# Late stores and the modulation's weight loads issued from GpSimd's queue instead of SP's, in a kernel of two transformer-like blocks

## The chip, the cores and the metric

The kernel runs on one core of a Trainium2 chip. The metric is the device time of the core in microseconds, from launch to end, the median of several runs; lower is better. TensorE multiplies matrices, VectorE (DVE) and ScalarE (ACT) work on whole tiles of 128 partitions, GpSimd (POOL) does the same more slowly, and SyncE (SP) does nothing but issue DMA transfers. An engine works through its own instructions in order; an instruction waits until the semaphores of those that it depends on are set. Every engine can issue transfers, and a transfer's issue instruction stands in the queue of the engine that issues it, so that it waits there for its data and holds up what is behind it.

## The reference

Two blocks in float32 over x [1024 tokens, 1024 features]. The first: a norm, one wide projection, a bidirectional gated delta rule with 4 heads beside windowed attention with sinks, both gated, and an output projection added to x. The second has a modulation: from a condition c, six vectors of 1024 (shift, scale and gate for the attention, and the same for the feed-forward).

```python
x = x + mix @ w_out                                   # first block's end
mod = silu(c) @ w_ada + b_ada                         # w_ada [1024, 6144]
sh1, sc1, g1, sh2, sc2, g2 = split(mod, 6)
h = rms_norm(x, norm1_g) * (1 + sc1) + sh1
gq, gk, gv, gr, glr, aq, ak, av = split(h @ w_in)
y_gla = gated_linear_attention(gq, gk, gv, gr, glr)
y_att = dilated_attention(rms_norm(aq), rms_norm(ak), av)   # 8 heads, 3 dilations
x = x + g1 * (concat(y_gla, y_att) @ w_out_2)
h = rms_norm(x, norm2_g) * (1 + sc2) + sh2
u = causal_conv(h @ w_up)                             # 2 x 2816 wide
x = x + g2 * ((silu(u_gate) * u_val) @ w_down)
```

## The kernel before

Activations lie transposed, features on partitions, as 128x512 tiles (two halves of the 1024 tokens). Every float32 product is made of three passes: each operand is split into a high part (ACT) and a low part (DVE), and TensorE adds high x high, high x low and low x high (mm3, L217 to L221). So each weight tile goes through a load, an ACT split and a DVE split (load_piece, L204 to L211: the load at L208 into one of two "wr" tiles, the splits at L209 and L210 into one of eight "wh" and "wl" tiles).

The stages, by the profile's times: first projections to 360 us; delta rule and windowed attention to 620; output projection 1 (out_proj, L322 to L393) to 727; second projections to 1105; dilated attention as filler from about 880 and the gated linear attention to 1285; output projection 2 to 1378; the up projection in 22 steps to 1800; the down projection to the end.

Transfers are issued in three queues, named at L117: `dma` is SP's, `store` is ACT's, `pdma` is POOL's. Before the change POOL's queue issues only the 28 stores of the delta rule's preparation (L678, L687, L714) between 258 and 321 us; nearly all others are SP's. The order in which each engine issues its instructions is not that of the program's text: a scheduler of the language lays it out ahead, with a timeline of its own, so that a transfer which moves to another queue can change the order elsewhere too. Transfers of one queue also rotate over completion semaphores, eight for the hardware queues and eight others for POOL's.

The places that the change touches:

- `ada` (L395 to L414) makes the modulation. Each of 12 steps j sums eight products of a 128x512 weight tile with a per-partition scalar: the first tile is loaded into the accumulator aac (L401) and scaled by ACT (L405), the other seven tiles wa are loaded (L401) and added by DVE (L403); then four small matmuls sum over partitions (pada, L412), and L414 puts the result into mods. Steps 0 to 3 run as filler in output projection 1; steps 4 to 11 are interleaved with the start of the second projections, two loads per step, with four 256 KB tiles for accumulator and weights together.
- L863 stores the delta rule's output yt (two buffers) to DRAM, 16 times 128 KB.
- `evac1` (L1080) adds output projection 1 to x and stores x1, 16 times 256 KB (L1082). The norm behind it (fin1, L1086 to L1093) scales x in place (L1088) and makes the second projections' inputs ho.
- L1260 stores a quarter of a head of the dilated attention, yd with one buffer, 32 times 64 KB; L1277 reads them back for output projection 2.
- `evac2` (L1620) and L1622 do for output projection 2 what evac1 does, with the modulation's gate: 16 stores of x2.
- `gated` (L1706) stores the activation of each of the 22 steps of the up projection, 512 KB each (L1721).

The up weights come in at L1576 (wu), are split at L1579 and L1580; the b tiles (b30l, b60l and so on) are sums of activations for the up projection's products, their low parts made at L1736. L1308 squares a tile of q or k on POOL for its norm, L1157 works on rotated q. L361 loads weights of the output projections (rawo, rawp).

Of the kernel before, what the change touches and what calls it, by code (L numbers as in the profile page):

```python
# [22 lines left out]
P = 128  # L23
# [89 lines left out]
def tile_two_blocks(ctx: ExitStack, tc: tile.TileContext, t, out, dbg=None, stop=None):  # L113
# [3 lines left out]
    dma, store, pdma = nc.sync.dma_start, nc.scalar.dma_start, nc.gpsimd.dma_start  # L117
# [18 lines left out]
    def after(*names):  # L136

        c = ExitStack()
        for n in names:
            c.enter_context(tc.issue_after(marks[n].ins))  # L140
        return c
# [253 lines left out]
    def ada(page, pbank, js):  # L395

        for j in js:
            aac = page("aac", f"aac{j}")
            for k in range(NK):
                wa = page("wa", f"wa{j}_{k}") if k else aac  # L400
                dma(wa, t["w_ada_2"][j, k])  # L401
                if k:
                    V.scalar_tensor_tensor(aac, wa, silc[:, k : k + 1], aac, ALU.mult, ALU.add)  # L403
                else:
                    A.activation(aac, aac, AF.Copy, scale=silc[:, 0:1])  # L405
                yield
            for _ in range(ADA_D):
                yield
            with after("mm3"):
                ps = pbank(f"pada{j}", [P, 4])  # L410
                for i in range(4):
                    T.matmul(ps[:, i : i + 1], aac[:, i * P : (i + 1) * P], ones, start=True, stop=True)  # L412
            md = mods[:, j // 2, 4 * (j % 2) : 4 * (j % 2) + 4]
            V.tensor_tensor(md, ps, md, ALU.add)  # L414
# [3 lines left out]
    ydram = scratch("ydram", [512, S])  # L418
# [4 lines left out]
    x1dram, x2dram = scratch("x1dram", [D, S]), scratch("x2dram", [D, S])  # L423
    mix = [[None, None] for _ in range(NK)]

    with ExitStack() as c1:
# [28 lines left out]
        with ExitStack() as ca:  # L455
# [4 lines left out]
            def page(tag, name, shape=None, dt=F32):  # L460
                return ga.tile(shape or [P, H], dt, name=name, tag=tag, bufs=BUFS_A[tag])
# [327 lines left out]
        with ExitStack() as cb_:  # L789
# [47 lines left out]
            def swa_values(b, g, sts, zt):  # L837
                kb0, kb1 = max(b - 1, 0), min(b + 2, NB)
                nm_ = f"{b}{g}"
                pts = []  # L840
                for i, kb in enumerate(range(kb0, kb1)):
                    pt = pb("pt", f"pT{nm_}{kb}", G4)
                    for h in range(4):
                        T.transpose(pt[:, h, :], sts[h][:, i * P : (i + 1) * P], ident)
                    pT = page("pTs", f"pTs{nm_}{kb}")
                    if PTS[kb % len(PTS)]:
                        A.activation(pT, pt, AF.Copy)
                    else:
                        V.tensor_copy(pT, pt)  # L849
                    pts.append(pT)  # L850
                    yield
                po = pb("po", f"po{nm_}", [P, 4, 64])
                for h in range(4):
                    for i, kb in enumerate(range(kb0, kb1)):
                        T.matmul(po[:, h, :], pts[i][:, h, :], sv[:, kb, g * 64 : (g + 1) * 64], start=i == 0, stop=kb == kb1 - 1)  # L855
                V.tensor_tensor(zt, zt, po, ALU.mult)
                yield
                pt = pb("pt", f"yp{nm_}", [P, 2, P])
                for i in range(2):
                    T.transpose(pt[:, i, :], zt[:, 2 * i : 2 * i + 2, :].rearrange("p a b -> p (a b)"), ident)  # L860
                yt = pg.tile([P, 2, P], F32, name=f"yt{nm_}", tag="wa", bufs=2)
                A.activation(yt, pt, AF.Copy)
                dma(ydram[g * 256 : (g + 1) * 256, b * P : (b + 1) * P].rearrange("(i p) s -> p i s", p=P), yt)  # L863
                yield

            def swa():
# [211 lines left out]
    with ExitStack() as co:  # L1078

        def evac1(xr, ps, m, cols):  # L1080
            V.tensor_tensor(xr, ps, xr, ALU.add)
            dma(x1dram[m * P : (m + 1) * P, cols], xr)  # L1082

        hs = [[None, None] for _ in range(NK)]

        def fin1(h, xs, rows, gsc, xp):  # L1086
            for k in range(NK):
                A.activation(xs[k], xs[k], AF.Copy, scale=gsc[:, k : k + 1])  # L1088
                V.tensor_tensor(xs[k], xs[k], rows, ALU.mult)
                hi, lo = hpage(f"ho{h}{k}h"), hpage(f"ho{h}{k}l")  # L1090
                A.activation(hi, xs[k], AF.Identity, bias=mods[:, 0, k : k + 1])
                V.scalar_tensor_tensor(lo, xs[k], mods[:, 0, k : k + 1], hi.bitcast(F32), ALU.add, ALU.subtract)
                hs[k][h] = (hi, lo)  # L1093

        order = (4, 5, 6, 7, 0, 1, 2, 3)
        ppo = pool(co, "ppo", space=PSUM)

        def modulation(xp):

            tiles = lambda tag, nm: xp.tile([P, H], F32, name=nm, tag=tag, bufs=dict(aac=2, wa=6)[tag])  # L1100
            return ada(tiles, lambda nm, shape: ppo.tile(shape, F32, name=nm, tag="nm", bufs=2), range(4))

        out_proj(co, ppo, t["w_out"], mix, t["xT"], evac1, "norm1_g_2", 0, "o", order, fin1, lambda: swa_mix(1), filler=modulation)
        free("O1")
        dump("x1", x1dram)
# [5 lines left out]
    yadram = scratch("yadram", [512, S])  # L1111
    mixg = [[None, None] for _ in range(4)]
    mixa = [[None, None] for _ in range(4)]
    with ExitStack() as c2:
# [75 lines left out]
        def attend(h, ready):  # L1190

            qs, kT, tb, vv, _ = ready
            for j in LASTJ if h == 7 else range(NB // 2):
# [58 lines left out]
                yd = rd = page("yd", f"ayd{h}{j}", [64, 2 * P])  # L1252
# [3 lines left out]
                else:  # L1256
                    A.activation(rd, po[64:128, : 2 * P], AF.Copy)
                    V.tensor_tensor(yd, po[0:64, : 2 * P], rd, ALU.add)
                    V.tensor_tensor(yd, yd, po[0:64, 2 * P :], ALU.mult)
                dma(yadram[h * 64 : (h + 1) * 64, j * 2 * P : (j + 1) * 2 * P], yd)  # L1260

        def heads(h0, h1):
            ready = {h0: prep(h0)}
# [19 lines left out]
        with ExitStack() as ca:  # L1283
# [120 lines left out]
            for nm in JOBS.split():  # L1404
                g = int(nm[-1])
# [159 lines left out]
    adram2 = scratch("adram2", [DFF, S])  # L1565
    with ExitStack() as cf:
# [52 lines left out]

        def evac2(xr, ps, m, cols):  # L1620
            V.scalar_tensor_tensor(xr, ps, mods[:, 2, m : m + 1], xr, ALU.mult, ALU.add)
            dma(x2dram[m * P : (m + 1) * P, cols], xr)  # L1622

        with after("exp", "red"):
            for j in range(2):
# [83 lines left out]
        def gated(j):  # L1709

            us = []
            c1, c2 = quarters.pop(j)
            for m, cc, tg in ((NFF + j, c2, "u"), (j, c1, "act")):
                u = page4(tg, f"u{m}", [P, S])
                A.activation(u, cc, AF.Identity, bias=fcb[:, m : m + 1], scale=fcw[:, m, 2:3])  # L1715
                for sft in (1, 2):
                    V.scalar_tensor_tensor(u[:, sft:], cc[:, : S - sft], fcw[:, m, 2 - sft : 3 - sft], u[:, sft:], ALU.mult, ALU.add)  # L1717
                us.append(u)
            A.activation(us[1], us[1], AF.Silu)
            V.tensor_tensor(us[1], us[1], us[0], ALU.mult)  # L1720
            dma(adram2[j * P : (j + 1) * P, :], us[1])  # L1721

        fcw = load(fw, "fcw", [P, 2 * NFF, 3], t["conv_w_2"])
        fcb = load(fw, "fcb", [P, 2 * NFF], t["conv_b_2"])
# [49 lines left out]
        for j in range(2):  # L1774
            gated(j)
# [55 lines left out]
        w1, w2, b = {}, {}, {}  # L1831
# [9 lines left out]
        for q in PROD_D:  # L1841
# [38 lines left out]
            for m in range(4):  # L1880
                p = ps[m]
# [3 lines left out]
                else:  # L1885
# [5 lines left out]
                    g, h = {2: (0, 0), 4: (1, 0), 5: (1, 1), 3: (0, 1)}[q]  # L1891
                    xr, dst = final(g, m, h, c, f"{q}{m}")
# [94 lines left out]
```

## Time and profile before

| | us |
|---|---|
| median of 3 runs | 2028.75 |
| lowest, highest | 2025.3, 2029.26 |
| the profiled execution | 2027.4 |
| its span, first to last instruction | 2025.6 |
| TensorE busy | 1938.5 |
| DVE busy | 1457.2 |
| ACT busy | 952.8 |
| POOL busy | 334.0 |
| mean granted clock | 0.978 |

TensorE's busy time is that of matmuls, which are pipelined. An issue instruction of a transfer is not counted as busy, so that a full queue of SP doesn't show in these numbers; it shows in the waits of SP's queue and in its timeline. Each wait is listed with what ended it.

### The profile page before, as it was taken

Reading aid. Unit: us, or ns where it says so; the run is one execution under the profiler, and the core shown is the slowest. Engines: PE = TensorE matmul, PEld = TensorE weight load, DVE = VectorE, ACT = ScalarE, POOL = GpSimd, SP = SyncE. Lnnn points to the kernel's source line nnn. Section 1 sums busy time; section 2 is a strip of 40 time slices with the busy share of each in tenths; the row PEclk is TensorE's granted clock in tenths of the full one; section 3 lists DMA queues with packets and bytes.
Section 4 is the critical chain, followed back from the end, with each engine's and each line's share of the span. In section 5 each row is a group of like instructions: output and inputs, shape, how many; then the busy total and the mean of one; then the engine's idle time right before and its main releaser. Section 6 shows DMA issues by size and latency. Waiting matters only on the chain.

```text
span 2025.6 us, 31441 instructions
## 1 busy us (share of the span) xinstructions
PE 1938.5 (96%) x11430; PEld 1683.3 (83%) x11430; DVE 1457.2 (72%) x3031; ACT 952.8 (47%) x1982; POOL 334.0 (16%) x389
## 2 busy tenths in 40 slices
PE   7999999899989998899999899999999999999999
PEld 6988889889977788798999787786888888888887
DVE  6797885587886478544354978449977777776987
ACT  6546563243353152125644566436554544554443
POOL 0000021563351123021022742110000000000000
PEclk9999999999999989899999999999999999999999
DMA  5232343325428327633222222611222222268332
GB/s 176 71 105 69 89 148 118 78 59 184 134 89 312 120 92 241 205 118 92 74 73 82 59 71 81 227 63 59 84 73 94 83 73 94 73 208 281 99 99 84
DMA packets 175996, 234.74 MB, mean 116 GB/s; under 512 B 57024, under 2 KB 93152, under 8 KB 175840
## 3 DMA queue, kind: packets, MB, share of 16 engines
q1 hardware_dynamic: 144800, 198.63, 30.9%
q10 hardware_dynamic: 28928, 27.27, 4.1%
q0 software_dynamic: 2112, 6.82, 1.0%
q8 instruction: 90, 1.47, 0.3%
q14 instruction: 66, 0.54, 0.1%
HBM read 174.47 MB, written 58.20 MB: 115 GB/s over the span
## 4 chain that ended last, share of the span: by engine, by line
PE 74%; DVE 12%; DMA 7%; ACT 3%; issue 3%; SPq 1%; POOL 0%; ACTq 0%; DVEq 0%; POOLq 0%
PE upx L220 4%; PE upx L221 4%; PE upx L219 4%; PE up L220 3%; PE up L221 3%; PE up L219 3%; DMA wa<-in_w_ada 2%; PE fm L219 2%; PE fm L221 2%; PE fm L220 2%; PE dnx L220 2%; PE dnx L219 2%; PE dnx L221 2%; PE po L855 1%; PE apo L1233 1%
## 5 line engine op out<-in xcount | busy, mean ns | idle before, releaser
L1579 ACT ACTIVATE uh<-wu 128x512 fp32r<-128x512 f32 x154 | 94.6, 628 | 143.1 <-DMA wu<-in_w_up 51.7
L1717 DVE SCALAR_TENSOR_TENSOR u<-c,fcw,u 128x1023 f32<-128x1023 f32 (+1 forms) x88 | 112.4, 1277 | 10.3 <-ACT u L1715 10.3
L1580 DVE TENSOR_TENSOR ul<-wu,uh 128x512 fp32r<-128x512 f32 x154 | 105.4, 696 | 4.1 <-ACT uh L1579 4.0
L210 DVE TENSOR_TENSOR wl<-wr,wh 128x512 fp32r<-128x512 f32 (+1 forms) x100 | 71.3, 720 | 39.5 <-ACT wh L209 39.2
L209 ACT ACTIVATE wh<-wr 128x512 fp32r<-128x512 f32 (+1 forms) x100 | 62.5, 630 | 71.7 <-PE fm L220 16.8
L403 DVE SCALAR_TENSOR_TENSOR aac<-wa,silc,aac 128x512 f32<-128x512 f32 x84 | 68.6, 817 | 33.8 <-DMA wa<-in_w_ada 29.7
L198 ACT ACTIVATE wdh<-w 128x512 fp32r<-128x512 f32 x55 | 34.8, 632 | 79.7 <-PE dnx L220 23.8
L591 DVE SCALAR_TENSOR_TENSOR cacc<-raw,cw,cacc 128x512 f32<-128x512 f32 x96 | 68.8, 744 | 1.7 <-ACT cacc L589 0.5
L220 PE MATMUL dnx<-bdl,wdh 128*128 128x512 f32 x176 | 68.6, 390 | 0.0
L221 PE MATMUL dnx<-bdh,wdl 128*128 128x512 f32 x176 | 68.5, 389 | 0.0
L1209 DVE CUSTOM_DVE_ANT_0 ass<-as,tb 128x512 f32<-128x512 f32 (+2 forms) x96 | 51.5, 552 | 23.1 <-PE as L1208 21.6
L1216 ACT ACTIVATE ass<-ass,amx 128x128 f32<-128x128 f32 (+3 forms) x64 | 49.2, 770 | 33.1 <-DVE amx L1215 31.1
L1715 ACT ACTIVATE u<-c,fcb,fcw 128x1024 f32<-128x1024 f32 x44 | 54.6, 1241 | 8.1 <-DVE c L1701 4.2
L199 DVE TENSOR_TENSOR bdl<-act,bdh 128x512 fp32r<-128x512 f32 x77 | 52.6, 684 | 1.8 <-ACT bdh L198 1.5
L220 PE MATMUL dny<-bdl,wdh 128*128 128x512 f32 x132 | 51.4, 389 | 0.0
L221 PE MATMUL dny<-bdh,wdl 128*128 128x512 f32 x132 | 51.4, 389 | 0.0
L828 ACT ACTIVATE ssb<-ssb,wnm 128x384 f32<-128x384 f32 (+1 forms) x64 | 36.8, 578 | 29.4 <-DVE wes L830 18.5
L1226 PE MATMUL apt<-ident,ass 128*128 128x128 f32 x288 | 47.7, 281 | 1.8 <-ACT ass L1216 1.3
L219 PE MATMUL dnx<-bdh,wdh 128*128 128x512 f32 x176 | 48.9, 390 | 0.4 <-DVE dp L1890 0.4
L855 PE MATMUL po<-sv,pTs 128*128 128x64 f32 x352 | 48.0, 277 | 1.4 <-DVE pTs L849 0.7
L198 ACT ACTIVATE bdh<-act 128x512 fp32r<-128x512 f32 x77 | 47.8, 620 | 2.1 <-issue 1.6
L855 PEld LDWEIGHTS po<-sv,pTs 128*128 128x128 f32 x352 | 46.3, 200 | 2.9 <-DVE pTs L849 1.4
(2159 smaller groups left out, 6907.4 us busy)
## 6 DMA issues: line engine op xcount, KB each, us to landing
wu<-in_w_up SPq DMA_DIRECT2D x44, 512.0 KB, 3.3
wa<-in_w_ada SPq DMA_DIRECT2D x84, 256.0 KB, 3.7
adram<-u SPq DMA_DIRECT2D x22, 512.0 KB, 2.8
act<-adram SPq DMA_DIRECT2D x44, 256.0 KB, 5.3
wd<-in_w_down SPq DMA_DIRECT2D x20, 512.0 KB, 3.6
wr<-in_w_in_fm SPq DMA_DIRECT2D x24, 256.0 KB, 2.8
w<-in_w_down SPq DMA_DIRECT2D x22, 256.0 KB, 5.4
xt<-in_xT SPq DMA_DIRECT2D x16, 256.0 KB, 5.2
```

The lines of the kernel that those rows point to most:

```text
L198: A.activation(hi, src, AF.Copy)
L209: A.activation(hi, raw, AF.Copy)
L210: V.tensor_tensor(lo, raw, hi.bitcast(F32), ALU.subtract)
L219: T.matmul(ps, ah, bh, start=first, stop=False, skip_group_check=more)
L220: T.matmul(ps, ah, bl, start=False, stop=False, skip_group_check=more)
L221: marks["mm3"] = T.matmul(ps, al, bh, start=False, stop=last, skip_group_check=more)
L403: V.scalar_tensor_tensor(aac, wa, silc[:, k : k + 1], aac, ALU.mult, ALU.add)
L591: V.scalar_tensor_tensor(acc, raw[h][:, j : j + H], cw[:, m, j : j + 1], acc, ALU.mult, ALU.add)
L855: T.matmul(po[:, h, :], pts[i][:, h, :], sv[:, kb, g * 64 : (g + 1) * 64], start=i == 0, stop=kb == kb1 - 1)
L1579: A.activation(hi, src, AF.Copy)
L1580: V.tensor_tensor(lo, src, hi.bitcast(F32), ALU.subtract)
L1717: V.scalar_tensor_tensor(u[:, sft:], cc[:, : S - sft], fcw[:, m, 2 - sft : 3 - sft], u[:, sft:], ALU.mult, ALU.add)
```

## The change

Six places call `pdma` where they called `dma`: 198 transfers move from SP's queue to POOL's. Sizes, tiles and data stay.

```diff
@@ ada (L401)
-                dma(wa, t["w_ada_2"][j, k])
+                pdma(wa, t["w_ada_2"][j, k])
@@ delta rule, output (L863)
-                dma(ydram[g * 256 : (g + 1) * 256, b * P : (b + 1) * P].rearrange("(i p) s -> p i s", p=P), yt)
+                pdma(ydram[g * 256 : (g + 1) * 256, b * P : (b + 1) * P].rearrange("(i p) s -> p i s", p=P), yt)
@@ evac1 (L1082)
-            dma(x1dram[m * P : (m + 1) * P, cols], xr)
+            pdma(x1dram[m * P : (m + 1) * P, cols], xr)
@@ dilated attention (L1260)
-                dma(yadram[h * 64 : (h + 1) * 64, j * 2 * P : (j + 1) * 2 * P], yd)
+                pdma(yadram[h * 64 : (h + 1) * 64, j * 2 * P : (j + 1) * 2 * P], yd)
@@ evac2 (L1622)
-            dma(x2dram[m * P : (m + 1) * P, cols], xr)
+            pdma(x2dram[m * P : (m + 1) * P, cols], xr)
@@ gated (L1721)
-            dma(adram2[j * P : (j + 1) * P, :], us[1])
+            pdma(adram2[j * P : (j + 1) * P, :], us[1])
```

## Rows read from the trace of the kernel before

**Rows 1.** The page's first part: busy time of each engine, its share of the span and its instructions.

```profile
PE 1938.5 (96%) x11430; PEld 1683.3 (83%) x11430; DVE 1457.2 (72%) x3031; ACT 952.8 (47%) x1982; POOL 334.0 (16%) x389
```

**Rows 2.** The windows: stretch in us, its length, busy time of PE, PEld, DVE, ACT and POOL with instructions in brackets, then the granted clock, the DMA engines' share and GB/s.

```profile
720.00:740.00 20.00, 16.83 (x98) 15.81 (x97) 11.28 (x29) 8.88 (x15) 0.50 (x1) 0.74 0.31 106
740.00:800.00 60.00, 55.09 (x440) 54.69 (x439) 57.18 (x111) 20.93 (x41) 21.81 (x21) 0.94 0.62 197
760.00:880.00 120.00, 105.50 (x748) 100.01 (x747) 80.96 (x155) 28.78 (x55) 21.24 (x15) 0.89 0.66 207
1100.00:1180.00 80.00, 71.44 (x490) 60.21 (x489) 64.84 (x164) 44.65 (x111) 59.46 (x90) 0.96 0.25 64
1320.00:1340.00 20.00, 20.00 (x96) 16.44 (x95) 4.58 (x17) 1.89 (x3) 1.30 (x1) 1.00 0.11 40
1380.00:1420.00 40.00, 35.19 (x143) 26.56 (x143) 37.90 (x73) 25.93 (x46) 0.00 (x0) 0.96 0.16 53
1420.00:1860.00 440.00, 440.00 (x1927) 361.38 (x1926) 336.99 (x434) 223.53 (x329) 0.00 (x0) 1.00 0.33 117
```

**Rows 3.** The waits of SP's queue over the whole span: line, what ended the wait, us in total, times, longest us.

```profile
SPq L1721 <- DVE u L1720: 143.3, 22, 13.9
SPq L1622 <- DVE xrp L1621: 68.4, 13, 8.6
...
SPq L1260 <- DVE ayd L1259: 44.2, 8, 14.9
SPq L1082 <- DVE xro L1081: 43.6, 10, 6.8
...
SPq L863 <- ACT yt L862: 14.4, 7, 7.4
```

**Rows 4.** The view of line 687, a 256 KB store issued by POOL: duration of the issue in ns (least, median, most), and us from issue to landing.

```profile
L687 POOL DMA_DIRECT2D adram<-ta x16: 540/542/551, 260.4 to 319.1; - x16
...
DMA to landing us min/median/max: 2.3/2.6/4.0
```

**Rows 5.** The same view of line 1082, a 256 KB store issued by SP.

```profile
L1082 SPq DMA_DIRECT2D x1dram<-xro x16: 319/326/327, 633.0 to 723.7; - x16
...
DMA to landing us min/median/max: 2.0/2.0/6.3
```

**Rows 6.** The timelines of POOL (the first two lines) and of DVE (the last four) from 276 to 290 us: start, us, instruction, and in brackets the idle time before it and what ended that.

```profile
277.26 1.14 POOL L687 DMA_DIRECT2D adram<-ta  x2 [0.57 <-DVE ta L686]
281.52 0.76 POOL L678 DMA_DIRECT2D mdram<-x  x1 [3.12 <-DVE x L677]
...
277.48 1.29 DVE L661 TENSOR_TENSOR rr<-tri,av 128x512 f32<-128x512 f32 x2
280.53 0.69 DVE L677 TENSOR_TENSOR x<-x,w 128x512 f32<-128x512 f32 x1
```

**Rows 7.** The timeline of SP's queue from 690 to 760 us; a line takes consecutive issues together, waits between them included.

```profile
700.52 23.45 SPq L1082 DMA_DIRECT2D x1dram<-xro  x5
724.02 15.29 SPq L208 DMA_DIRECT2D wr<-in_w_aq  x8
```

**Rows 8.** The timeline of ACT from 718 to 742 us.

```profile
727.02 1.32 ACT L209 ACTIVATE wh<-wr 128x512 fp32r<-128x512 f32 x2 [0.57 <-DMA wr<-in_w_aq]
732.13 0.63 ACT L209 ACTIVATE wh<-wr 128x512 fp32r<-128x512 f32 x1 [3.78 <-DMA wr<-in_w_aq]
```

**Rows 9.** Groups of DVE instructions from 740 to 800 us: count, busy us, mean ns, and idle time before them.

```profile
L210 DVE TENSOR_TENSOR wl<-wr,wh 128x512 fp32r<-128x512 f32 (+1 forms) x10 | 8.5, 851 | 0.0
```

**Rows 10.** The chain of waits in 750 to 890 us: shares of the stretch by line.

```profile
by line: DMA wa<-in_w_ada 24.8%; DVE aac L403 10.6%; issue 8.2%; PE ak L219 4.7%; PE ak L220 4.5%; PE ak L221 4.4%; DVE wl L210 3.9%; DMA aac<-in_w_ada 3.3%; DMA wr<-in_w_av 3.1%; DVE ayq L1315 3.0%; PE pla L1351 2.7%; DMA wr<-in_w_ak 2.6%;
```

**Rows 11.** The waits of all engines in 750 to 890 us: us in total, times, longest us.

```profile
POOL asqk L1308 <- ACT ayk L1305: 74.5, 3, 64.2
DVE aac L403 <- DMA wa<-in_w_ada: 27.3, 23, 3.2
...
PE pada L412 <- DVE aac L403: 8.5, 4, 3.4
```

**Rows 12.** The view of line 401, the modulation's loads on SP's queue: their landing, least, median and most.

```profile
DMA to landing us min/median/max: 2.5/3.7/7.2
```

**Rows 13.** POOL's longest wait in 1100 to 1290 us (the first line), and the issues of line 1260 in 1100 to 1180 us (the second).

```profile
POOL spq L1157 <- ACT spq L1156: 40.0, 2, 32.6
...
L1260 SPq DMA_DIRECT2D yadram<-ayd x8: 451/451/1411, 1106.2 to 1172.4; - x8
```

**Rows 14.** The timeline of SP's queue at the end of the attention.

```profile
1262.18 9.66 SPq L1260 DMA_DIRECT2D yadram<-ayd  x2
...
1282.09 0.45 SPq L1260 DMA_DIRECT2D yadram<-ayd  x1
```

**Rows 15.** The waits of PE in 1270 to 1420 us.

```profile
PE p L219 <- ACT ma30h L1278: 3.4, 1, 3.4
PE upx L220 <- DVE b60l L1736: 2.4, 1, 2.4
PE up L220 <- DVE b30l L1736: 1.4, 1, 1.4
```

**Rows 16.** The timeline of SP's queue in output projection 2.

```profile
1302.38 53.08 SPq L1622 DMA_DIRECT2D x2dram<-xrp  x10
1355.51 0.92 SPq L1576 DMA_DIRECT2D wu<-in_w_up  x2
```

## The prediction

> **What bounds the kernel now.** I read the page first: TensorE is busy 96% of the span [rows 1], so only the remaining 87 us (2025.6 - 1938.5) can be won, and only where TensorE idles. Next the windows by stage [rows 2]: from 1420 to 1860 us TensorE is busy 440.00 of 440.00, so nothing that any queue does there can be worth anything. It idles 14.5 us of 120 in 760:880, 8.6 of 80 in 1100:1180, 4.8 of 40 in 1380:1420, and 3.2 of 20 in 720:740, at a lower granted clock (0.74) as well. Then SP's queue [rows 3], which shows what the moved stores hold up: it stands 143.3 us at L1721, 68.4 at L1622, 44.2 at L1260 for one of its writers, 43.6 at L1082, 14.4 at L863, each time because it has reached a store whose data is not computed yet. A wait of a queue costs nothing by itself; what counts is which load stands behind it, and whether TensorE is waiting for that load.
>
> **What one move costs.** 198 transfers go from SP to GpSimd's queue (POOL): 96 loads at L401, 16 stores at L863, 16 at L1082, 32 at L1260, 16 at L1622, 22 at L1721. A POOL-issued store of 256 KB exists already: 542 ns on the queue and 2.6 us to landing [rows 4]; SP's of the same size takes 326 ns and 2.0 us [rows 5]. POOL starts 0.30 us after its producer: DVE's L677 ends at 280.53 + 0.69 = 281.22, POOL's L678 starts at 281.52 [rows 6]. By the medians a moved transfer lands 0.30 + 0.22 + 0.6 = 1.1 us later at most, by the least landings (2.3 and 2.0) 0.30 + 0.22 + 0.3 = 0.8; I take 0.8, as some of the first sum's landing is the other transfers' doing. POOL's 198 x 0.55 = 109 us more of queue time fit in a queue that is 16% busy [rows 1], stage by stage except where said below. Does a POOL transfer slow DVE? Beside two POOL issues (277.26, 1.14 us) two DVE operations take 1.29 us [rows 6], 0.65 each, against 0.69 for one alone in the same rows: no price. Nor does a busy DVE stretch POOL's issue: the sixteen of L687 lie between 540 and 551 ns [rows 4], in a stage where DVE works on 128x512 tiles.
>
> **Term 1, out projection 1 to the second projections: -5 us (0 to -8).** SP reaches five x1 stores at 700.52 and stands there 23.45 us; the first weights of the second projections (wr, L208) follow at 724.02 [rows 7]. They wait for nothing but their place: the queue goes on with all eight in 15.29 us. ACT, which splits them, then waits 0.57 and 3.78 us for two of them [rows 8], and TensorE gets 16.83 us of work out of 20 at 0.74 clock [rows 2]. With the stores on POOL the wr loads are due about 20 us earlier, as soon as a slot is free; the eight DVE splits that go with them (851 ns each beside the rest, 6.8 us [rows 9]) can go before 720, out of 740:800, where DVE is busy 57.18 of 60 [rows 2]. The gain is the 3.2 idle us, the clock's part of the 20 us, and some of those splits: between 3.2 and 8. I take 5. What is late next is the chain of the second norm's half on DVE. Zero is the lower end: that chain may end where it does now.
>
> **Term 2, the modulation's loads, 754 to 873 us: 0 (-4 to +15).** Here the change does not take a store away, it moves loads with a consumer right behind. Of the chain in 750:890, DMA wa is 24.8% and aac 3.3% [rows 10], some 39 of 140 us; DVE waits 27.3 us for wa, and TensorE 8.5 for the sums made of them [rows 11]. SP issues a load as its slot falls free, and it lands 3.7 us later [rows 12]. With 0.8 us more on 3.7 the 39 us become 39 x 0.8 / 3.7 = 8.4 longer, if nothing gives way. For the move speaks that SP no longer mixes these loads with wr loads whose slots are not free, so either kind can pass the other, and that POOL has nothing to issue between 803 and 867: it waits 64.2 us for ACT at L1308 [rows 11]. Against it, POOL issues in order: a load that is laid behind one of its waits (the other two waits of that group come to 10 us) holds up DVE's next addition, and with it all of DVE. The order of each engine is laid out ahead by a scheduler with a timeline of its own, which can place DVE's additions later, as x2's sums use the result first at 1302 [rows 16]. So I take 0, between a gain of 4 (half of TensorE's 8.5 us) and 8.4 plus one uncovered POOL wait of 6.
>
> **Term 3, y stores of the first block (L863), -1 (-4 to +2).** SP's 14.4 us there hold back weights of out projection 1 [rows 3]; I take a fourteenth, and at most a fourth (4), since seven waits share them and other weights are in flight; against it, POOL is already at work in that stage, and two of the stores may stand 1 us behind its operations. **Term 4, attention stores (L1260), +1 (-1 to +6).** In 1100:1180 POOL is busy 59.46 of 80 [rows 2], and from 1100 to 1290 it waits 40.0 us in two pieces for ACT [rows 13]: a store behind such a wait keeps the one output tile occupied, and the next head's ACT and DVE operations wait for it; eight stores [rows 13] x 0.55 us more on POOL is 4.4, and one wait behind which a store is caught takes the upper end to 6. **Term 5, end of the attention, -1 (-3 to +1).** SP stands 9.66 us at two stores from 1262.18, with out projection 2's weights behind; but the last store goes out at 1282.09 when its data is there [rows 14], and TensorE's 3.4 us wait for the mix that reads it back [rows 15] gets the 0.8 us later landing. **Term 6, out projection 2 to the up projection, -2 (-6 to 0).** Ten x2 stores hold SP for 53.08 us from 1302.38, and the two next up weights go at 1355.51 [rows 16]. Loaded earlier, their splits could use DVE while it is busy 4.58 of 20 (1320:1340) and not 37.90 of 40 (1380:1420) [rows 2], where TensorE waits 2.4 and 1.4 us for DVE [rows 15]. All that TensorE idles there is 4.8 us, and DVE's relief may carry 1 more; some of the split tiles come free late, so I take 2. **Term 7, up projection's 22 stores: 0.** The 143.3 us are the largest wait that goes, and TensorE is never idle beside it.
>
> **Sum.** -5 + 0 - 1 + 1 - 1 - 2 + 0 = -8 us. The profiled execution took 2027.4 us, 1.35 under the median of 2028.75 (runs 2025.3 to 2029.26); from the median it gives 2020.75, so 2021. A rule speaks against it: the Trainium skill (DMA: Bandwidth & Descriptors, Issuing engines are not separate DMA queues) says that transfers of all engines share the same 16 DMA engines, and that another issuer saves only sequencer time, usually small. By it the time would stay. The rows on issue time agree (326 ns a store), but the rows on waits show another thing that goes, a load's place behind a store that isn't ready.
>
> **Rivals.** *Slower, the loads' latency (2036).* Between 754 and 873 the slot-to-slot round of the modulation's loads sets the pace: each lands 0.8 us later (+8.4), and two of POOL's waits are not covered by the slots in flight (+6). Less term 1 (-5) and half of terms 3 to 6 (-2): +7. It decides as soon as DVE has no other work to put between two loads. For it: 24.8% of that chain, DVE's 27.3 us. Against: DVE and TensorE have other work there, and the loads are not urgent. *No change (2028).* The stores' places were hidden: DVE, near full from 740 to 800, ends the norm where it does now, and what term 1 gains is waited for again in 760:880. For it: the share of DVE there. Against: ACT's separate waits for wr. The rule of the Trainium skill above, from the page DMA: Bandwidth & Descriptors, would give this time too. *Larger gain (2010).* Term 1 at -8, term 2 at -4, term 3 at -3, term 6 at -4: -19. For it: TensorE's idle in these stages is over 30 us. Against: each end at once.
>
> **Chances.** Forecast 0.45 (its own range 2014 to 2027), latency 0.27, no change 0.16, larger gain 0.12. A measurement of this kernel tells 0.2%, 4 us, from no change. Faster by more: most of the forecast and the larger gain, 0.50. Within: 0.22. Slower: most of the latency rival and a little of the forecast's failures, 0.28. The range runs from 2006 (below the larger gain, by the lower ends) to 2038 (the latency rival with term 4 at +3).
>
> **What would show it.** Right: wr loads issued before 715 on SP; TensorE near 20 of 20 and clock 1.00 in 720:740; the up weights issued between 1300 and 1350; TensorE's waits for b60l and b30l gone; the up stage as long as before. Wrong: DVE's wait for wa above 40 us, the last L403 later than before against the end of the norm, POOL waits ahead of L401 issues; more DVE or ACT waits for yd; no TensorE gap closed in 720:740 or 1380:1420.

## The result, and the profile after

The changed kernel takes 2056.7 us (median of 4 runs, 2048.55 to 2059.9) where the kernel before, on the same chip, takes 2029.01 (2025.3 to 2031.11). The ratio is 1.0131, 95% interval 1.0113 to 1.0150: 27 us slower, where 8 us faster was forecast, and outside the range. The profiled execution took 2057.2 us with a span of 2055.4.

```profile
PE 1943.3 (95%) x11430; PEld 1685.8 (82%) x11430; DVE 1469.1 (71%) x3031; ACT 951.5 (46%) x1982; POOL 442.6 (22%) x587
```

The busy times [rows 1 for before] say little: DVE is 12 us busier, POOL 109. POOL's number, unlike SP's, does hold the issue instructions of its transfers, against what the section on the time before says of all of them: 198 instructions more (389 to 587) at 0.55 us make these 109. Where the time went is found by matching matmuls: a matmul that writes the same tile in both traces, and how much later it ends in the trace of after. Only changes of this number along the span are losses or gains.

| stage (time in the kernel before, us) | after minus before at its end, us | change |
|---|---|---|
| to the end of the first block's attention, 610 | 0.4 | |
| start of out projection 1, to 680 (14.5 at 640, of which 6 come back) | 8.4 | +8.0 |
| rest of it and the step to the second projections, to 745 | 7.5 | -0.9 |
| modulation beside the second projections, to 920 | 9.1 | +1.6 |
| rest of the projections, to 1100 | 9.1 | 0 |
| the scan of the gated linear attention, to 1200 | 26 to 28 | +18 |
| end of the attention, out projection 2, to 1380 | 28 | 0 |
| start of the up projection, to 1400 | 30 | +2 |
| the rest | 29.4 | -0.7 |

Two stages carry it, and neither is one on which the forecast's gains rested. The windows of after (those from 1110 on moved along with the delay; columns as in [rows 2]):

```profile
620.00:640.00 20.00, 8.03 (x30) 5.53 (x30) 9.60 (x14) 5.58 (x10) 7.04 (x13) 0.75 1.01 369
720.00:740.00 20.00, 16.84 (x80) 14.17 (x79) 12.47 (x27) 11.74 (x21) 5.95 (x6) 0.89 0.18 63
760.00:880.00 120.00, 103.47 (x769) 98.01 (x768) 78.56 (x158) 29.07 (x56) 55.02 (x79) 0.91 0.65 200
1110.00:1190.00 80.00, 60.05 (x367) 50.25 (x366) 64.58 (x130) 33.83 (x85) 52.36 (x77) 0.83 0.20 53
1400.00:1440.00 40.00, 33.93 (x146) 26.22 (x145) 33.97 (x66) 21.67 (x38) 2.60 (x3) 0.96 0.11 40
1440.00:1880.00 440.00, 439.43 (x1923) 360.45 (x1922) 342.05 (x442) 225.17 (x334) 11.76 (x22) 1.00 0.32 111
```

TensorE has 8.03 us of work in 620:640 (19.69 before) and 60.05 of 80 in the scan (71.44 in the like stretch of before), at a granted clock of 0.83 there against 0.96. In 720:740, where the largest gain was forecast, it stands at 16.84, against 16.83 before. The up stage stays full, so that the 22 stores there cost nothing, as forecast.

**The scan.** Its POOL part begins with a run of eight operations at L1460 and ends with the last L1482; between them POOL scales q and k level by level (L1480, L1481), DVE and ACT copy q into qb (L1472), TensorE makes the scores (ps, L1446), and the next level begins. The views of the two lines give first and last start, before (first fence) and after (second):

```profile
L1460 POOL TENSOR_TENSOR sc<-ident,dg x8: 1037/1088/1216, 1108.7 to 1116.0; 128x512 f32<-128x512 f32 x8
...
L1482 POOL TENSOR_TENSOR pre<-pre x28: 211/364/700, 1128.6 to 1190.5; 128x256 f32<-128x256 f32 x4, 128x128 f32<-128x128 f32 x4, 128x64 f32<-128x64 f32 x4, 128x32 f32<-128x32 f32 x4
```

```profile
L1460 POOL TENSOR_TENSOR sc<-ident,dg x8: 1030/1031/1041, 1118.3 to 1125.3; 128x512 f32<-128x512 f32 x8
...
L1482 POOL TENSOR_TENSOR pre<-pre x28: 208/321/606, 1140.8 to 1218.1; 128x256 f32<-128x256 f32 x4, 128x128 f32<-128x128 f32 x4, 128x64 f32<-128x64 f32 x4, 128x32 f32<-128x32 f32 x4
```

The scan grew from 81.8 to 99.8 us, the whole 18. POOL's waits within it, before and then after:

```profile
POOL gk L1481 <- PE ps L1446: 11.3, 8, 6.6
POOL spk L1157 <- ACT spk L1156: 4.8, 2, 3.6
```

```profile
POOL yadram L1260 <- DVE ayd L1259: 16.0, 2, 14.3
POOL spk L1157 <- ACT spk L1156: 3.2, 2, 3.0
POOL yadram L1260 <- DVE ayd L1255: 2.9, 2, 2.0
```

Before, POOL waits for the scan's own scores. After, it waits 19 us at the attention's stores, and one of these waits alone is 14.3 us; the scan's next scaling of q starts only behind it (POOL's timeline):

```profile
1140.76 2.32 POOL L1482 TENSOR_TENSOR pre<-pre 128x256 f32<-128x256 f32 x4
1157.35 0.57 POOL L1260 DMA_DIRECT2D yadram<-ayd  x1 [14.27 <-DVE ayd L1259]
1157.93 0.87 POOL L1480 TENSOR_TENSOR gq<-gq,pre 128x256 f32<-128x256 f32 x1
```

Something else is new. A DVE copy of 64x256 takes 7.92 us where the same line took 0.29 to 1.10 before (timelines of DVE, before and after):

```profile
1111.81 1.10 DVE L1472 COPY qb<-gq 64x256 f32<-64x256 f32 x1
1113.67 0.29 DVE L1472 COPY qb<-gq 64x256 f32<-64x256 f32 x1
```

```profile
1119.46 7.92 DVE L1472 COPY qb<-gq 64x256 f32<-64x256 f32 x1
...
1140.00 3.10 DVE L1214 TENSOR_TENSOR amx<-amx 128x1 f32<-128x1 f32 x1
```

The first ends 0.15 us behind POOL's run of 1118.28 to 1127.23 (the eight of L1460 and two fills behind them), the second 0.02 behind POOL's L1482 in the timeline above (1140.76 + 2.32 = 1143.08): DVE was kept out until POOL had nothing more to do. In the scan of the kernel before, no DVE operation waits so over more than one of POOL's. The Trainium skill (SBUF — State Buffer, SBUF: two separate sides) has the ports that the two share as a lock held for a whole instruction; here it lasted for a run of instructions.

The 14.3 us are not all lost to the store. Before, POOL stands at the same place too, for the scores:

```profile
1138.41 0.86 POOL L1481 TENSOR_TENSOR gk<-gk,pre 128x256 f32<-128x256 f32 x1 [6.59 <-PE ps L1446]
```

And after, the scores are late themselves. TensorE's first scores and those of the second level, before (first fence) and after (second):

```profile
1111.31 0.60 PE L1446 MATMUL ps<-qb,gk 128*128 128x128 f32 x4
...
1134.58 0.80 PE L1446 MATMUL ps<-qb,gk 128*128 128x128 f32 x4
```

```profile
1127.52 1.20 PE L1446 MATMUL ps<-qb,gk 128*128 128x128 f32 x4 [7.20 <-DVE qb L1472]
...
1151.68 5.60 PE L1446 MATMUL ps<-qb,gk 128*128 128x128 f32 x32
```

Counted from the first L1460 (1108.67 and 1118.28), the first scores begin at 2.6 us before and at 9.2 after, 6.6 later, because the q copy that they need is the one of 7.92 us. The second level's begin at 25.9 and 33.4, 7.5 later, and POOL's next L1481 starts at 29.7 and 40.5 (1158.74), 10.7 later. So up to here some 7 of the 18 us go back to the long copy and about 3 to the store's wait; the rest comes in the later levels.

**The start of out projection 1.** TensorE waits 11.3 us for a weight tile (its waits in 600 to 660; 1.7 before):

```profile
PE o L219 <- ACT who L364: 11.3, 1, 11.3
```

That tile is split by ACT, whose timeline shows what stands before it:

```profile
629.43 0.63 ACT L1062 ACTIVATE my01h<-my01l 128x512 fp32r<-128x512 f32 x1 [7.46 <-DMA my01l<-ydram]
635.52 0.63 ACT L1062 ACTIVATE my11h<-my11l 128x512 fp32r<-128x512 f32 x1 [5.46 <-DMA my11l<-ydram]
...
637.19 1.99 ACT L364 ACTIVATE who<-rawo 128x1024 fp32r<-128x1024 f32 x2
```

ACT waits in order for two tiles that are read back from the store of L863. In after the last of these stores lands 7.0 us after its issue, among seven loads in flight and seven more issued in the next 4 us; before, 1.9, with two in flight. But the late landing alone does not make the loss: with the modulation's loads alone on POOL (a run below) the last store, still SP's, takes 6.8 us, and TensorE waits 1.6. There ACT's order is another one. L863's landing (least, median, most) and ACT's timeline in that run:

```profile
DMA to landing us min/median/max: 1.9/2.4/6.8
```

```profile
622.28 1.04 ACT L364 ACTIVATE who<-rawo 128x1024 fp32r<-128x1024 f32 x1
...
628.03 1.06 ACT L364 ACTIVATE who<-rawo 128x1024 fp32r<-128x1024 f32 x1 [4.09 <-DMA rawo<-in_w_out]
628.99 0.61 ACT L1062 ACTIVATE my11h<-my11l 128x512 fp32r<-128x512 f32 x1
```

The second weight split (622.28) and the third stand ahead of my11h, as in the kernel before. In after the second stands behind it, at 637.19, though its weights, issued at 608.14, had landed by 614.1. Only in this order does the late landing hold TensorE up.

### The profile page after: what moved, and what is told of

Read it like the earlier page. It is cut to its first block, busy times and chain, and to the rows that moved or that the text cites. A ratio compares the mean times of both kernels' runs of the same rounds, so it can differ in the third digit from the quotient of the medians.

```text
span 2055.4 us, 31482 instructions
## 1 busy us (share of the span) xinstructions
PE 1943.3 (95%) x11430; PEld 1685.8 (82%) x11430; DVE 1469.1 (71%) x3031; ACT 951.5 (46%) x1982; POOL 442.6 (22%) x587
## 4 chain that ended last, share of the span: by engine, by line
PE 74%; DVE 13%; DMA 5%; issue 4%; ACT 3%; POOL 1%; SPq 0%; ACTq 0%; DVEq 0%; POOLq 0%
PE upx L219 4%; PE upx L220 4%; PE upx L221 4%; PE up L220 3%; PE up L221 3%; PE up L219 3%; PE fm L219 2%; PE fm L221 2%; PE fm L220 2%; PE dnx L220 2%; PE dnx L219 2%; PE dnx L221 2%; PE dny L219 1%; PE o L219 1%; PE dny L220 1%
## 5 line engine op out<-in xcount | busy, mean ns | idle before, releaser
L1721 POOL DMA_DIRECT2D adram<-u x22 | 11.8, 534 | 437.8 <-DVE u L1720 437.8
L209 ACT ACTIVATE wh<-wr 128x512 fp32r<-128x512 f32 (+1 forms) x100 | 62.4, 630 | 80.9 <-PE fm L220 16.4
L403 DVE SCALAR_TENSOR_TENSOR aac<-wa,silc,aac 128x512 f32<-128x512 f32 x84 | 71.5, 851 | 36.2 <-DMA wa<-in_w_ada 25.4
L401 POOL DMA_DIRECT2D wa<-in_w_ada x84 | 45.6, 544 | 79.4 <-DVE aac L403 55.1
L1715 ACT ACTIVATE u<-c,fcb,fcw 128x1024 f32<-128x1024 f32 x44 | 54.6, 1240 | 8.0 <-DVE c L1701 4.3
```

The lines of the kernel that those rows point to most:

```text
L209: A.activation(hi, raw, AF.Copy)
```

## The experiments

Each is timed against the kernel before on its own chip; "scan" is the time from the first L1460 to the last L1482, as above. The edits are against the kernel before, or against the changed kernel where said.

**All but the attention stores** (changed kernel):

```diff
-                pdma(yadram[...], yd)
+                dma(yadram[...], yd)
```

> The whole change with the attention stores of L1260 back on SP. Theory A (the attention stores on POOL's in-order queue, and what they do to DVE beside POOL, cost the 18 us that the traces lose between 1105 and 1180): about 2037 to 2040, and no DVE instruction there that waits over several POOL instructions in a row (after had 7.9, 3.7 and 3.1 us). Theory B (the 18 us come of any new order of the engines, whichever part is moved): 2050 to 2060.

2040.08, ratio 1.0057 (1.0039 to 1.0075); scan 80.9; no DVE operation kept out over several of POOL's. By the ratios 15 us of the loss are the attention stores', and theory A holds so far.

**The attention stores alone:**

```diff
-                dma(yadram[...], yd)
+                pdma(yadram[...], yd)
```

> Only the attention stores of L1260 are on POOL. Theory A: 2043 to 2050, lost between 1100 and 1190, with long DVE instructions beside POOL's runs again. Theory B: within 5 us of before, 2024 to 2034.

2044.18, ratio 1.0079 (1.0052 to 1.0107); scan 100.7; DVE operations of 7.89, 3.06, 2.24 and 2.01 us. Alone the stores lose 16 us, about the 15 that the whole change loses by them. (The execution with this trace took 2057.0 us, the longest of eight.)

**All but the modulation's loads** (changed kernel):

```diff
-                pdma(wa, t["w_ada_2"][j, k])
+                dma(wa, t["w_ada_2"][j, k])
```

> The whole change with the modulation's loads of L401 back on SP. If these loads on POOL cost what the drift shows (7 us at the start of out projection 1, 620 to 660, and about 7 net after 820): 2040 to 2046. If the drift of 620 to 660 comes of the stores of L863 and L1082 instead: 2050 to 2058.

2045.9, ratio 1.0080 (1.0051 to 1.0109), scan 100.1, with a DVE copy of 7.90 us again. Nothing is lost to 680 (0.4), and at 920 the kernel is 2.5 us ahead of before: with these loads on SP, the rest loses only in the scan.

**The modulation's loads alone:**

```diff
-                dma(wa, t["w_ada_2"][j, k])
+                pdma(wa, t["w_ada_2"][j, k])
```

> Only the modulation's loads of L401 are on POOL. If they cost the time at 620 to 660 and 840 to 905: 2034 to 2045, with TensorE's wait of over 8 us at the start of out projection 1 as in after. If they do not: 2024 to 2032.

2024.01, ratio 0.9983 (0.9963 to 1.0003): no loss; a gain of 3 is not told from no change. So the loads' latency is not the price, against the rival "slower". By themselves they do not make the loss at 620 either; it needs a partner.

**The modulation's loads with x1, x2 and the up projection's stores:** L401, L1082, L1622, L1721 as in the changed kernel, L863 and L1260 left on SP.

```diff
-                dma(wa, t["w_ada_2"][j, k])
+                pdma(wa, t["w_ada_2"][j, k])
...
-            dma(x1dram[m * P : (m + 1) * P, cols], xr)
+            pdma(x1dram[m * P : (m + 1) * P, cols], xr)
```

> On POOL: the modulation's loads and the stores of x1, x2 and the up projection; the stores of L863 and L1260 stay on SP. If the loss at the start of out projection 1 (6 us at 620 to 660) needs the y stores of L863 on POOL as well: 2020 to 2028, without TensorE's wait of over 8 us there. If the x1 stores make it: 2036 to 2044 as with all but L1260 moved.

2031.54, ratio 1.0027 (1.0011 to 1.0044), at 680 level with before (-0.1): x1's stores are not the partner. That this version is 5 us slower is clear of the interval, and not traced to a stage: its profiled execution ends 0.8 us behind that of before.

**The modulation's loads with the y stores:**

```diff
-                dma(wa, t["w_ada_2"][j, k])
+                pdma(wa, t["w_ada_2"][j, k])
...
-                dma(ydram[...], yt)
+                pdma(ydram[...], yt)
```

> On POOL: the modulation's loads and the y stores of L863, nothing else. If the two together make the loss at the start of out projection 1: 2028 to 2032, 5 to 7 above the loads alone (2024), with TensorE's wait there. If x1's stores are needed as well: 2022 to 2026.

2035.11, ratio 1.0048 (1.0033 to 1.0063), by the ratios 13 us above the loads alone, where 5 to 7 were expected. TensorE's waits in 600 to 640 here, and then in the run with the loads alone (600 to 650):

```profile
PE o L219 <- ACT who L364: 11.8, 1, 11.8
```

```profile
PE o L219 <- ACT who L364: 1.6, 1, 1.6
```

So the pair makes it: the store of L863 in POOL's queue beside the modulation's loads. In all runs with both (after, this one, and four with other edits) TensorE waits 8.8 to 11.9 us, and ACT's second weight split stands behind my11h; in those with one of them it waits 3 at most, and the split stands ahead. That the order and not the landing makes the wait is read from these traces; no run has both moves with the split ahead.

**One POOL transfer more, ahead of the scan's first run:**

```diff
             for q_ in qb[0] + qb[1]:
-                G.memset(q_, 0.0)
+                marks["qb"] = G.memset(q_, 0.0)
+            with after("qb"):
+                pdma(scratch("gdump", [P, 32]), dg.rearrange("p a b c d -> p (a b c d)"))
```

> The kernel before with one POOL transfer more, a 16 KB store of the scan's diagonal to scratch, issued just ahead of the eight L1460 operations; the order up to there is the same on every engine. Theory D (a POOL transfer shortly ahead lets a run of POOL operations keep DVE out until the run ends): the first DVE copy qb beside the run takes 6 to 8 us and not 0.3 to 1.1, and the time is 2034 to 2042. Theory E (the long DVE operations come of the new order alone): no DVE operation beside POOL waits over more than one POOL operation, 2026 to 2032.

2031.3, ratio 1.0023 (1.0011 to 1.0035): 4.7 us, scan 89.6. Timelines of DVE and then of POOL:

```profile
1111.01 7.83 DVE L1474 COPY qb<-gq 64x256 f32<-64x256 f32 x1
```

```profile
1109.15 0.58 POOL L1436 DMA_DIRECT2D gdump<-dg  x1
1109.75 8.01 POOL L1462 TENSOR_TENSOR sc<-ident,dg 128x512 f32<-128x512 f32 x8
```

A transfer of 16 KB that waits for nothing makes the long copy, as theory D says, and costs 4.7 us; the time itself lies below D's 2034 and within E's range. As the whole cause D does not survive the other runs, below.

**All qb copies on ACT**, in the changed kernel and, as its base, in the kernel before:

```diff
-QB = (0, 1)
+QB = (0, 0)
```

> The whole change, with all copies into qb (L1472, L1474) on ACT and none on DVE. If DVE's waits beside POOL are what the attention stores cost (12 to 14 us of DVE, 9 of them at the qb copies): 2040 to 2048, by 14 at most above the same edit of the kernel before. If the cost is the scan's POOL operations that stand behind a store: 2052 to 2060.

> The kernel before, with all copies into qb on ACT: the base for the run above. Either theory: 2022 to 2034.

Changed: 2056.62, ratio 1.0155 (1.0131 to 1.0179), scan 91.8. Before: 2021.04, ratio 0.9980 (0.9967 to 0.9994), scan 78.5. The edit does not spare the changed kernel anything, by time; but the long wait moves to the next DVE operations (L1214, 6.29 us, and a cast at L1429, 6.60), so that DVE is kept out as before and the run does not tell the two explanations apart. The 4 us that the base gains are a by-product.

**POOL waits for the attention's tile, but issues no transfer:**

```diff
+                G.tensor_tensor(pg.tile([1, 1], F32, name=f"seen{h}{j}", tag="seen"), yd[0:1, 0:1], yd[0:1, 0:1], ALU.mult)
                 dma(yadram[...], yd)
```

> The kernel before, its attention stores on SP; ahead of each store POOL multiplies one element of the output tile by itself (32 operations of 1x1), so that POOL waits in order for the tile as it does with the store in its queue, but issues no transfer. If POOL's waits in order for the attention's output hold up the scan: 2036 to 2046, most of the 16 us that the attention stores alone cost on POOL. If the transfers on POOL are what costs: 2026 to 2032.

2043.31, ratio 1.0065 (1.0042 to 1.0088): about the loss that the stores alone make (1.0079), but not in the same place. The scan is 92.3 us, 10.5 more than before, where the stores make 18.9 more; TensorE loses another 7 us between 1240 and 1320, where the last outputs are waited for. That the totals agree is in part luck. The runs also fall into two groups, 2035 to 2036 and 2043 to 2045, so the size is loose. POOL's waits in the scan:

```profile
POOL gk L1482 <- PE ps L1447: 7.1, 6, 2.4
POOL gk L1482 <- ACT ayd L1254: 6.6, 1, 6.6
POOL seen L1260 <- DVE ayd L1259: 6.2, 2, 4.4
```

So no transfer is needed for most of the cost. Nor for long DVE operations, if shorter ones: there are four of 2.8 to 3.5 us, with no transfer on POOL for over 700 us before them (its own 28 stores end at 343 us, a little later than said of the kernel before), and one of 3.32 in the run with loads and y stores, where POOL issues none in the scan. What decides whether POOL lets DVE in between two operations is not settled.

**Fourteen POOL transfers that wait for nothing**, ahead of each half level of the scan:

```diff
+                        with after("run") if "run" in marks else nullcontext():
+                            pdma(gdump[(2 * l + h) * P : (2 * l + h + 1) * P], dg.rearrange("p a b c d -> p (a b c d)"))
                         for m in range(2):
                             q4, k4, e4 = v4(gq[m]), v4(gk[m]), v4(pres[m])
...
-                            G.tensor_tensor(tot(1), tot(0), tot(1), ALU.mult)
+                            marks["run"] = G.tensor_tensor(tot(1), tot(0), tot(1), ALU.mult)
```

(The memsets of qb set the mark "run" first; gdump is a scratch tensor.)

> The kernel before with 14 POOL transfers more, 16 KB stores to scratch of a tile that is ready long before, one ahead of each half level of the scan; nothing to wait for. If transfers on POOL ahead of its runs of operations keep DVE out and that is most of the 16 us: three or more DVE operations of 2 to 8 us and 2036 to 2046, 5 to 15 more than with the single one. If one transfer's 5 us are all that this can cost: 2029 to 2033.

2035.09, ratio 1.0051 (1.0033 to 1.0069); scan 99.8, with DVE operations of 8.73 and 2.08 us. The scan stretches as in after, but part of it is won back: this trace enters the scan 4.3 us ahead of before and ends 6.2 behind, 10.5 in all, as the ratio says. The price of transfers alone is thus 5 to 10 us, less than the 16 of the attention stores.

**Only the eight stores inside the scan on SP** (changed kernel), and **only these on POOL:**

```diff
-                pdma(yadram[...], yd)
+                (dma if h in (3, 4) else pdma)(yadram[...], yd)
```

```diff
-                dma(yadram[...], yd)
+                (pdma if h in (3, 4) else dma)(yadram[...], yd)
```

> The whole change, but the 8 stores of heads 3 and 4, which fall into the scan of the gated linear attention, are back on SP; the other 24 attention stores stay on POOL. If the stores inside the scan make the loss: 2037 to 2043, as with all 32 on SP (2040), and the scan's POOL part 80 to 86 us long. If the others or the mere new order make it: 2050 to 2058 and 95 us or more.

> The kernel before with only the 8 stores of heads 3 and 4 on POOL. If they make the loss: 2040 to 2046, as with all 32 on POOL (2044), the scan's POOL part 95 to 102 us. If not: 2024 to 2032 and 80 to 86 us.

Back on SP: 2045.64, ratio 1.0078 (1.0054 to 1.0103), scan 86.5: 11 us of the loss go, though the long copy stays (7.92 us). So the long copy by itself stretches the scan by some 5 us here. On POOL alone: 2029.18, ratio 1.0004 (0.9988 to 1.0019), scan 83.0, POOL's waits at the stores 7 us and not 19: no loss. The same eight stores cost 11 us in one order and nothing in the other.

**The extra transfer and the eight stores together** (against the kernel before, the two edits shown above), and **head 2's four stores on SP** (changed kernel):

```diff
-                pdma(yadram[...], yd)
+                (dma if h == 2 else pdma)(yadram[...], yd)
```

> The kernel before with the one extra 16 KB POOL store ahead of the scan's first POOL run and with the 8 stores of heads 3 and 4 on POOL. If the two work upon each other: 2040 to 2046, the scan's POOL part 95 us or more, POOL waiting 15 us or more for the stores' data. If they only add (5 and 1): 2031 to 2035, 86 to 91 us.

> The whole change, but the 4 stores of head 2, the last of which stands just ahead of the scan's first POOL run, are back on SP; the stores of heads 3 and 4 inside the scan stay on POOL. If the long wait of DVE beside that run is what makes the stores cost: no DVE operation of 7 us, the scan 81 to 88 us, 2038 to 2044. If the stores inside the scan cost in the new order without it: 95 us or more, 2050 to 2057.

Together: 2035.51, ratio 1.0059 (1.0036 to 1.0081), scan 91.6, where the parts gave 4.7 + 0.8 = 5.5 us and the pair 12 (7 to 16): more than the sum of the medians, but the intervals meet, and scan and time stay below what was expected if the two work upon each other (95 us, 2040). Head 2 on SP: 2047.64, ratio 1.0109 (1.0074 to 1.0144), scan 92.4, the long copy gone, two DVE operations of 3.71 and 3.86 us. By the scan's length, head 2's stores make 7 of the 18 us and the eight inside it 13. Neither is the one cause. By time, what goes with the long copy is 4 to 5 us three times over (4.7 in the kernel before with the extra transfer, 4.3 from the run without attention stores on POOL to the one with only the eight on SP, 4.5 from this run to after), and the eight stores inside the scan make 11 (after less the run with them on SP; this run less the one without any attention store gives 10.5). Single differences of 4 to 5 us are within the noise of most of these intervals; that three agree, and that 4.5 and 10.5 add up to the 15 of all attention stores, is the evidence.

**Only x1's and x2's stores on POOL**, the bearers of terms 1 and 6:

```diff
-            dma(x1dram[m * P : (m + 1) * P, cols], xr)
+            pdma(x1dram[m * P : (m + 1) * P, cols], xr)
...
-            dma(x2dram[m * P : (m + 1) * P, cols], xr)
+            pdma(x2dram[m * P : (m + 1) * P, cols], xr)
```

> Only the stores of x1 and x2 (L1082, L1622) on POOL. By the forecast's terms 1 and 6: 7 us faster, 2019 to 2022. If the loads that they let pass are not what TensorE waits for, as the trace of after suggests (the same waits for wr and for b60l as before): 2024 to 2029.

2031.37, ratio 1.0018 (0.9996 to 1.0040): no gain. SP's queue, ACT and the windows of this run:

```profile
694.48 43.33 SPq L208 DMA_DIRECT2D wr<-in_w_aq  x8
...
1296.42 1.00 SPq L1576 DMA_DIRECT2D wu<-in_w_up  x2
```

```profile
725.76 0.72 ACT L1088 ACTIVATE xro<-xro,gsco 128x512 f32<-128x512 f32 x1 [2.03 <-DMA x1dram<-xro]
726.39 1.13 ACT L209 ACTIVATE wh<-wr 128x512 fp32r<-128x512 f32 x2
730.91 0.63 ACT L209 ACTIVATE wh<-wr 128x512 fp32r<-128x512 f32 x1 [3.39 <-DMA wr<-in_w_aq]
```

```profile
720.00:740.00 20.00, 16.83 (x114) 15.91 (x113) 11.57 (x31) 7.07 (x13) 0.56 (x1) 0.83 0.28 92
1380.00:1420.00 40.00, 34.65 (x145) 26.23 (x145) 37.22 (x63) 26.60 (x47) 0.00 (x0) 0.99 0.17 53
```

The loads do go out early, the weights of the second projections at 694 and not 724, the up weights at 1296 and not 1355. It helps nothing: ACT splits the first two at 726.39, as before at 727.02 [rows 8], because in its order they stand behind the last scaling of x, which waits for the store of x to land; the other six need the two slots that these two hold. TensorE has the 16.83 us of [rows 2] in 720:740, and 34.65 against 35.19 in 1380:1420.

**A candidate to beat both**, loads on POOL and the qb copies on ACT:

```diff
-QB = (0, 1)
+QB = (0, 0)
...
-                dma(wa, t["w_ada_2"][j, k])
+                pdma(wa, t["w_ada_2"][j, k])
```

> A candidate to beat both: the modulation's loads on POOL and all copies into qb on ACT, all stores on SP. If the gains of the two (4 and 5 us) add: 2016 to 2020. If the new order takes them back: 2022 to 2030.

2022.19, ratio 0.9989 (0.9973 to 1.0005): not told from no change. Of all versions only the qb copies on ACT alone are below before beyond the interval (0.9980).

## Why the prediction was wrong, point by point

**Term 4 is the step that failed** (+1, bounds -1 to +6; measured +18 in the scan in after, 16 for the stores alone). The text asked what a store loses by standing behind a POOL wait, and counted the eight stores' issue time, 4.4 us. It did not ask the reverse: what stands behind the store, and who waits for that. The wait for ACT that it took as the danger, 40.0 us in two pieces [rows 13], is not in the scan: the longer piece ends at 1104.94, ahead of the first L1460, the other lies at 1198, behind the last L1482. Within the scan POOL is a link of a chain, level after level, and its idle time there is the wait for the other links; a wait set into its order lengthens the chain. The run without a transfer (1.0065) shows that the waits and the order that goes with them are enough for most of it; the runs with waitless transfers show that POOL's and DVE's operations getting into each other's way adds to it. By the traces and times above the long copy is about 5 of the 15 or 16 us and the stores inside the scan about 11. That holds for the order of after alone: the same eight stores cost 11 us there and nothing in the order of the kernel before, and why is not settled.

**Term 3** (-1, at most +2; measured +8.0). The y store was priced as if alone. Moved with the modulation's loads, it lands in 7.0 us and not 1.9, and in ACT's new order the weight split that TensorE needs stands behind its reading back, so that TensorE waits 11.3 us. Alone neither part costs this, though with the loads alone the store lands as late (6.8). The forecast named the new order of the engines as a risk for the modulation only.

**Term 1** (-5; measured -0.9 from 680 to 745, and nothing with x1 and x2 alone). "They wait for nothing but their place" was right of the loads and wrong of what follows: the split's place in ACT's order is set by the scaling of x, and two slots hold back the other six. The term's own lower end, that the norm's chain ends where it does now, is what came. ACT's waits for the store's landing, 0.77 and 1.44 us in the kernel before, are one of 2.03 in after.

```profile
734.77 0.72 ACT L1088 ACTIVATE xro<-xro,gsco 128x512 f32<-128x512 f32 x1 [2.03 <-DMA x1dram<-xro]
735.40 1.13 ACT L209 ACTIVATE wh<-wr 128x512 fp32r<-128x512 f32 x2
739.92 0.63 ACT L209 ACTIVATE wh<-wr 128x512 fp32r<-128x512 f32 x1 [3.39 <-DMA wr<-in_w_aq]
```

**Term 2** (0, -4 to +15; measured +1.6 in after, and no change that can be told with the loads alone). Right in size, as a net. The last addition at L403 moves from 873.2 to 904.2 us, as the latency rival said. Inside the stage the matched matmuls gain first and lose again: 7.5 us behind at 745, 2.4 at 820, 9.1 at 905, and in the run with the loads alone 3.8 ahead, 12.4 ahead at 840, 5.6 ahead at 900; with these loads on SP (the rest as in the changed kernel) 2.8 us are gained to 820 and kept. So part of the rival's price seems to have been paid, and a gain of its size hid it; no run separates the two.

**Terms 5 and 6** (-1 and -2; measured 0 and +2). The weights came early, but the operands that TensorE waits for are not weights. After, 1280 to 1450:

```profile
PE p L219 <- ACT ma30h L1278: 2.7, 1, 2.7
PE upx L220 <- DVE b60l L1736: 2.4, 1, 2.4
PE up L220 <- DVE b30l L1736: 1.4, 1, 1.4
```

These are the waits of [rows 15], to the tenth in the up stage: sums of activations, which need x2's norm. **Term 7** (0) holds.

**The rivals.** The side came out as the one of the rival "slower" (0.27), but not by its mechanism, so by luck: the loads alone lose nothing, and the time was 20 us above its 2036. "No change" (0.16) comes closest to the fate of terms 1 and 6, though not by DVE's share: what was let past was waited for again at the next operation in order. The rule of the Trainium skill that another issuer saves only sequencer time (DMA: Bandwidth & Descriptors, Issuing engines are not separate DMA queues) agrees with x1 and x2 alone (1.0018, not told from 1); of the 27 us lost it says nothing.

## What to carry to other kernels

Before a store moves to another engine's queue, read what that engine does next and who waits for it: an engine that is idle between the links of a chain has no room for a wait, however low its busy share. A load that gains its place in a queue gains time only if its consumer's order and slots let it; look at what the consumer waits for besides. And price moved transfers together and read the order of the engines anew: here two moves that cost nothing one by one put a weight split behind a tile that is read back late.

## What the runs showed of the hardware

A DVE operation on SBUF tiles can be kept out by POOL for a whole run of operations, 7.8 to 7.9 us beside the eight of L1460 and 8.7 beside a later run, and not only for the one under way (1.1 us at most for the same copies in the kernel before). Waits of this length were seen only with a transfer on POOL shortly ahead (the one extra store brings one about, 7.83 us); shorter ones over several operations come without any (3.3 and 3.5 us). A 128 KB store landed in 1.9 us with two loads in flight, in 7.0 from POOL's queue with seven, and in 6.8 from SP's with nine.
